# Start of a decoder trunk step: more filler products, another buffer for two loads, an earlier gather

## The chip, the cores and the metric

The kernel runs on one core of one Trainium2 chip. The metric is the device time of one execution in microseconds (us); less is better. The kernel before has a median of 1006.9 us over three runs (1005.82 to 1008.11).

## The reference

One layer of a hybrid decoder is run for a prompt of 512 tokens and for 8 samples of one token each; both share the weights. All is float32.

```python
def trunk_layer(x, c, conv_buf, h0, pos0, attend, ...):
    sh1, sc1, g1, sh2, sc2, g2 = ada_modulation(c, ada_w, ada_b)      # silu(c) @ ada_w + ada_b, six parts
    h = rms_norm(x, norm1_g) * (1.0 + sc1) + sh1
    z = h @ w_in
    xr, gr, q, k, v, fl, ga, gb = jnp.split(z, cuts, axis=-1)
    ...   # branch A: convolution, RG-LRU, gelu gate, @ w_proj_a
    logf = jax.nn.log_sigmoid((fl + b_f).astype(jnp.float32))
    yb = attend(q, k, v, logf).reshape(B, T, ATTN_W) @ w_proj_b       # samples: cache_logf[page_table] too
    x = x + g1 * ((sigmoid(ga) * ya + sigmoid(gb) * yb) @ w_o)
    ...   # second norm, SwiGLU, residual; final norm
```

The model width D is 1024, the feed-forward width 2816, 16 heads of 64. The samples attend to 1024 past rows each, in pages of 128 rows; `cache_logf` is gathered by the page table.

## The kernel before, in words

Activations lie transposed: eight tiles of 128 features by 520 columns (512 prompt tokens, 8 samples), called `x[f]`, `xn[f]` (normed), `h[f]` (modulated). A full-precision product is made of three TensorE products, since each operand is split in a high and a low part (`whi`/`wlo` for weights, `hh`/`hl` for h): ScalarE rounds the high part, VectorE subtracts for the low one. TensorE then runs through one long list of such products; weights come by DMA in chunks and are split ahead of their use.

Instructions are written in program order, and a scheduler of the framework orders each engine's queue from it, by its own model of when operands are ready; each engine then works through its queue in that fixed order and waits at its head. All weight loads go through SyncE's (SP's) queue.

The start, which the change touches, is in this order:

- SP loads `par1` (norm and conditioning rows), the eight tiles of x, some constants, and then the adaLN weights. The modulation of the first norm is made in three parts (`first_mod`, parts 0, 1, 2: features 0 and 1, 2 and 3, 4 to 7). Parts 0 and 1 take four tiles each, two row blocks (`kq`) per tile; part 2 takes eight loads, one per row block.
- The sum of squares: for each f ScalarE squares `x[f]` (line 594) and VectorE adds it to `sq` (line 596). Ten products with one column each (`ss`, line 604) sum over the partitions; then come a root, a reciprocal, five small diagonal tiles `dg` (line 610), the products that spread the reciprocal over all partitions (`r`, line 615), and the copies of it to `r1`.
- Beside the squares `keep_busy` issues filler products into a bank that nobody reads (`idle`, line 509): ones times `x[f]`, 260 columns, float32, which the chip runs as two matmul instructions each. Each waits for the one before, and for the load of `x[f]`.
- `first_mod(0)` (line 489) stands on TensorE in two halves, ahead of and behind the products for `r`. Then `first_mod_end(0)`: copy, transpose (followed by two more fillers), `mod`, `n1amp`. Then `first_h(0)` and the first query products (`qa`, line 574).
- Parts 1 and 2 of the modulation follow between query products (lines 489 and 502), and `first_h(4)` to `first_h(7)` come after the end of part 2. Each `first_h` has two small operations on GpSimd (POOL) for the 8 sample columns (lines 538 and 539).

Three pools of buffers matter. `pgp` has 7 tiles of 4 KB per partition; nearly all early loads use it. `wp` with tag `wraw` has 2 tiles of 8 KB per partition, taken in turn: first two for query weights (`qraw`), the third for the last two row blocks of part 2 (`both`), the fourth for `lfp` (the gathered log f of the past), the fifth for the first weight chunk. `heap` has 60 tiles of 520 columns, handed out by `slot`.

`past_load` (line 439) is an indirect DMA, issued by POOL: it gathers 64 rows of the log f cache by `idx`, which a small DMA loads from the page table; `ptb` is the same table for page loads. The gathered rows are used by the transposes `lft` (line 451) in `past_turn`.

Of the kernel before, what the change touches and what calls it, by code (L numbers as in the profile page):

```python
# [67 lines left out]
def kernel(ctx, tc, xT, par1, par, gates, b_f, cst, cse, own, cache_k, cache_v, cache_lf, pt,  # L68
# [3 lines left out]
    pe, act, dve, pool, sp = nc.tensor, nc.scalar, nc.vector, nc.gpsimd, nc.sync  # L72
# [9 lines left out]
    def slot(name, cols=NT, dt=F32, parts=128):  # L82
        return heap.tile([parts, cols], dt, name=name, tag="slot")

    def bank(name, parts=128, cols=512):
        return psp.tile([parts, cols], F32, name=name, tag="bank")
# [76 lines left out]
    for jt in range(FF // 128):  # L163
        c = len(chunks)
# [4 lines left out]
        for name in BLOCKS:  # L169
            units.append((c, name, 4))  # L170
            if name in JOIN[jt]:
                g, i = JOIN[jt][name]
# [32 lines left out]
    def load_chunks(upto):  # L205
        while state["dma"] < len(chunks) and state["dma"] <= upto:
            c = state["dma"]
            if c in joined:
                raw = pgp.tile([128, GROUP, 256], F32, name="wraw", tag="pg")
            else:  # L210
                raw = wp.tile([128, KT, 256], F32, name="wraw", tag="wraw", bufs=2)
            o = 0
            for src, r0, nk, c0, n in chunks[c]:
                sp.dma_start(raw[:, :nk, o:o + n],
                             src[r0:r0 + nk * 128, c0:c0 + n].rearrange("(k p) c -> p k c", p=128))
                o += n
            raws[c] = raw
            state["dma"] += 1
# [214 lines left out]
    ptb = keep.tile([1, NS * NPAGE], I32, name="ptb")  # L433
    idx = keep.tile([NS * NPAGE, 1], I32, name="idx")
    lfp = []

    def past_load():
        t = wp.tile([NS * NPAGE, 2048], F32, name="lfp", tag="wraw", bufs=2)
        pool.indirect_dma_start(out=t, out_offset=None, in_=cache_lf,
                                in_offset=bass.IndirectOffsetOnAxis(ap=idx[:, 0:1], axis=0),  # L440
                                bounds_check=NPOOL - 1)
        lfp.append(t.rearrange("p (k h) -> p h k", h=H))
# [36 lines left out]
    def first_mod(part, acc, kqs):  # L479
        if part < 2:  # L480
            for kq in range(kqs[0], kqs[-1], 2):
                raw = pgp.tile([128, 2, 512], F32, name="araw", tag="pg")
                for v in range(2):
                    c0 = 1024 * v + 256 * part
                    sp.dma_start(raw[:, :, 256 * v:256 * v + 256],
                                 ada_w[kq * 128:kq * 128 + 256, c0:c0 + 256].rearrange("(k p) c -> p k c", p=128))
                for k in range(2):
                    for g in range(4):
                        m = pe.matmul(acc[32 * g:32 * g + 32, :128], lhsT=silc[:, kq + k],
                                      rhs=raw[:, k, 128 * g:128 * g + 128],  # L490
                                      start=kq + k == 0, stop=kq + k == KT - 1, tile_position=(0, 32 * g))
            return
        for kq in kqs:
            if kq < 6:
                raw = pgp.tile([128, 2, 512], F32, name="araw", tag="pg")
            else:
                if kq == 6:
                    both = wraw().rearrange("p (a k) c -> p a (k c)", a=2)
                raw = both[:, kq - 6].rearrange("p (v c) -> p v c", v=2)
            sp.dma_start(raw, ada_w[kq * 128:kq * 128 + 128, :2048].rearrange("p (v c) -> p v c", v=2)[:, :, 512:])  # L500
            for g in range(4):
                pe.matmul(acc[32 * g:32 * g + 32, :256], lhsT=silc[:, kq],
                          rhs=raw[:, g // 2, 256 * (g % 2):256 * (g % 2) + 256],
                          start=kq == 0, stop=kq == KT - 1, tile_position=(0, 32 * g))

    def keep_busy(m, n, f=0):
        for _ in range(n):
            with tc.issue_after(m.ins) if m is not None else nullcontext():
                m = pe.matmul(idle[:, :HALF], lhsT=ones, rhs=x[f][:, :HALF], start=True, stop=True)
        return m  # L510

    def first_mod_end(part, acc):
        nb = 1 if part < 2 else 2
        sb = slot("adas", 256)
        mods = act.copy(sb[:, :128 * nb], acc[:, :128 * nb])
        tp = bank(f"adaft{part}")
        for b in range(nb):
            m = pe.transpose(tp[:, b * 128:b * 128 + 128], sb[:, b * 128:b * 128 + 128], ident)
        if part == 0:
            keep_busy(m, 2)  # L520
        f0, nf = ((0, 2), (2, 2), (4, 4))[part]
        fs = slice(f0, f0 + nf)
        tv = tp[:, :128 * nb].rearrange("p (b g c) -> p b g c", b=nb, g=4)
        for v in (1, 0):
            dve.tensor_tensor(
                mod[:, v, fs].rearrange("p (q b) c -> p b q c", b=nb), tv[:, :, 2 * v:2 * v + 2, 0:9],
                prm1[:, fs, P_AB + v:P_AB + v + 1].rearrange("p (q b) c -> p b q c", b=nb).to_broadcast([128, nb, 2, 9]),
                ALU.add)
        amps = dve.scalar_tensor_tensor(amp1[:, fs], mod[:, 1, fs], 1.0,
                                        prm1[:, fs, P_N1:P_N1 + 1].to_broadcast([128, nf, 9]), ALU.add, ALU.mult)  # L530
        return mods, amps
# [21 lines left out]
    def q_split(kp, raw, g3, behind=(), mid=None):  # L553
        hi = wp.tile([128, 2, 384], F32R, name="whi", tag="whi", bufs=3)
        lo = wp.tile([128, 2, 384], F32R, name="wlo", tag="wlo", bufs=3)
        with ExitStack() as st:
            for b in behind:
                st.enter_context(tc.issue_after(b.ins))
            for k in range(0, 2, 1 if mid else 2):
                ks = slice(k, k + 1 if mid else 2)  # L560
                state["act"] = act.copy(hi[:, ks], raw[:, ks])
                if k:
                    st.enter_context(tc.issue_after(mid()[1].ins))
                state["last"] = dve.tensor_tensor(lo[:, ks], raw[:, ks], hi[:, ks].bitcast(F32), ALU.subtract)
        for k in range(2):
            for n in range(3):
                qw[2 * kp + k, g3 + n] = hi[:, k, 128 * n:128 * n + 128], lo[:, k, 128 * n:128 * n + 128]
# [9 lines left out]
    def wraw():  # L577
        return wp.tile([128, KT, 256], F32, name="wraw", tag="wraw", bufs=2)
# [6 lines left out]
    def q_step(ks, g3, k, banks, n0=0, n1=6):  # L585
        for n in range(n0, n1):
            q_matmuls(ks, g3 + n // 2, n % 2, k, banks[n])
# [4 lines left out]
    for f in range(KT):  # L592
        t = slot("sq1")
        act.activation(t, x[f], AF.Square)
        if f:
            dve.tensor_tensor(sq, sq, t, ALU.add)
        else:
            sq = t
        if 0 < f < 6:
            m = keep_busy(m, 1, f)  # L600
    NB = NT // 5
    ps = bank("ss1", NB, 5)
# [6 lines left out]
    for b in range(5):  # L609
        dve.tensor_scalar(dg[:, NB * b:NB * b + NB], ident[:NB, :NB], rt[:, b:b + 1], None, ALU.mult)  # L610
    first_mod(0, acc[0], range(0, 4))
    r1 = slot("r1")
    for j, (t0, t1) in enumerate(((0, 3 * NB), (3 * NB, NT))):
        ps = bank(f"r1_{j}")[:, :t1 - t0]
        pe.matmul(ps, lhsT=ones[:NB, :], rhs=dg[:, t0:t1], start=True, stop=True)
        act.copy(r1[:, t0:t1], ps)
    first_mod(0, acc[0], range(4, KT))
    qraw = {}

# [21 lines left out]
    q_step((0, 1), 0, 0, banks)  # L641
    q_step((0, 1), 0, 1, banks)
    first_mod(1, acc[1], range(0, 4))
    for n in range(6):
        t0, t1 = HALVES[n % 2]
# [22 lines left out]
    banks = [bank(f"qc{i}_{j}") for i in range(3) for j in range(2)]  # L668
    q_step(range(2, KT), 0, 2, banks)
    first_mod(2, acc[2], range(6, 8))  # L670
    q_split(2, qraw[2, 0], 0)
    first_mod_end(2, acc[2])
    q_step(range(2, KT), 0, 3, banks)
# [7 lines left out]
        q_step(range(2, KT), 0, k, banks)  # L681
    qbanks = banks
    sp.dma_start(prm, par)
    sp.dma_start(ptb, pt.rearrange("a b -> (a b)")[None, :])
    sp.dma_start(idx, pt.rearrange("a (b c) -> (a b) c", c=1))
    for kp in (2, 3):
        q_loads(kp, 3)
        q_split(kp, qraw[kp, 3], 3, ends)
    past_load()
    load_chunks(0)  # L690
    flr = slot("flr", KT * 32).rearrange("p (k c) -> p k c", k=KT)
    pool.memset(flr, 0.0)
# [332 lines left out]
    for i in range(KT):  # L1025
        if i % 4 == 0:
            qtp.append(bank(f"qt{i}", NS))
        if i < 6:
            t = qpart[i]
            for j, (t0, t1) in enumerate(HALVES):  # L1030
                if i < 3:
                    b = qbanks[2 * i + j]
                else:
                    b = bank(f"q{i}_{j}")
# [57 lines left out]
    g = [None] * KT  # L1092
# [397 lines left out]
    g = None  # L1490
# [340 lines left out]
    for j in range(2):  # L1831
        for m in range(2 * PLAIN):
            if j == 0:
                begin(u + 3)
            b = bank(f"fi{m}_{j}")
# [90 lines left out]
```

## Time and profile before

| what | value |
|---|---|
| median of three runs | 1006.9 us (1005.82 to 1008.11) |
| the profiled execution's own time | 1008.05 us |
| its span, first to last instruction | 1006.4 us |
| PE (TensorE) busy | 987.9 us, 98% |
| DVE (VectorE) busy | 789.2 us, 78% |
| ACT (ScalarE) busy | 566.2 us, 56% |
| POOL busy | 340.0 us, 34% |
| HBM read and written | 203 GB/s over the span |

Some 1.65 us of the execution's time lie outside the span. Busy time of PE is the union of its matmuls as the profile models them, so 98% says that it hardly stood still, not that it ran at its peak.

### The profile page before, as it was taken

What the parts mean: (1) busy time and instruction counts of PE and PEld (TensorE: products, weight loads), DVE (VectorE), ACT (ScalarE), POOL (GpSimd) and SP (SyncE); (2) the same over time, 40 slices, a digit from 0 to 9 for tenths busy, and PEclk for the clock granted to TensorE, in tenths of its full rate; (3) what the DMA queues carried; (4) which work ended last, traced back from release to release, by engine and by line L of the source; (5) the groups of instructions that cost most, each with busy time, mean ns of one, the idle gap of its engine ahead of it and who ended that gap; (6) DMA issues with size and microseconds to landing.
All of it is one profiled execution on the core that took longest, in us unless ns stands there. A gap on an engine that the chain in (4) does not pass through costs nothing.

```text
span 1006.4 us, 21548 instructions
## 1 busy us (share of the span) xinstructions
PE 987.9 (98%) x8090; PEld 917.0 (91%) x8090; DVE 789.2 (78%) x1410; ACT 566.2 (56%) x1165; POOL 340.0 (34%) x436
## 2 busy tenths in 40 slices
PE   6999999999999999999999999999999999999997
PEld 5899999999898988888888888999999999999996
DVE  4488999979999888887665454869888888888864
ACT  5443779876952477777782233554444444445453
POOL 0163121323244255644400001494343442433212
PEclk9999999999999999999999999999999999999999
DMA  9898756889879999997767995333324243233222
GB/s 320 294 291 300 230 198 183 272 260 304 266 237 371 321 312 279 320 283 235 250 208 260 334 338 151 86 97 93 106 84 126 66 125 100 69 106 105 64 63 86
DMA packets 165883, 206.14 MB, mean 205 GB/s; under 512 B 9986, under 2 KB 128402, under 8 KB 165714
## 3 DMA queue, kind: packets, MB, share of 16 engines
q1 hardware_dynamic: 149538, 153.24, 49.0%
q0 software_dynamic: 12560, 45.10, 13.2%
q10 hardware_dynamic: 3680, 6.42, 1.7%
q8 instruction: 63, 1.03, 0.4%
q14 instruction: 42, 0.34, 0.1%
HBM read 191.64 MB, written 13.09 MB: 203 GB/s over the span
## 4 chain that ended last, share of the span: by engine, by line
PE 87%; ACT 5%; DVE 4%; issue 2%; DMA 1%; POOL 0%; SPq 0%; DVEq 0%; POOLq 0%; ACTq 0%
PE fo L311 13%; PE wo L311 5%; PE pb L311 4%; PE gb L311 4%; PE k L311 4%; PE ga L311 4%; PE v L311 4%; PE xr L311 3%; PE pa L311 3%; PE pv L942 3%; PE gr L311 2%; PE po L1415 2%; PE ada L378 2%; PE ptt L1381 2%; PE fi L311 1%
## 5 line engine op out<-in xcount | busy, mean ns | idle before, releaser
L250 ACT CAST whi<-wraw 128x1024 fp32r<-128x1024 f32 (+1 forms) x79 | 82.2, 1040 | 97.5 <-PE pb L311 34.5
L252 DVE TENSOR_TENSOR wlo<-wraw,whi 128x1024 fp32r<-128x1024 f32 (+1 forms) x79 | 99.7, 1262 | 19.7 <-ACT whi L250 17.4
L274 ACT CAST wb<-ws 128x512 fp32r<-128x512 f32 x72 | 44.8, 622 | 88.9 <-PE fo L311 61.9
L311 PE MATMUL fo<-ach,wb 128*128 128x260 f32 x512 | 93.3, 282 | 0.0
L311 PEld LDWEIGHTS fo<-ach,wb 128*128 128x128 f32 x512 | 78.9, 188 | 0.0
L275 DVE TENSOR_TENSOR wb<-wraw,wb 128x512 fp32r<-128x512 f32 x86 | 74.5, 866 | 4.9 <-ACT wb L274 4.0
L265 POOL TENSOR_TENSOR ws<-wraw 128x512 f32<-128x512 f32 x18 | 23.8, 1324 | 152.9 <-DMA wraw<-in_w_fi_dram 94.8
L311 PE MATMUL fo<-acl,wb 128*128 128x260 f32 x256 | 72.3, 282 | 0.0
L275 DVE TENSOR_TENSOR wb<-ws,wb 128x512 fp32r<-128x512 f32 x72 | 61.1, 849 | 13.9 <-ACT wb L274 12.4
L274 ACT CAST wb<-wraw 128x512 fp32r<-128x512 f32 x86 | 53.5, 623 | 32.2 <-ACT cp L1813 6.2
L790 POOL DMA_DIRECT2D pg<-in_cache_k_dram x70 | 37.8, 540 | 100.2 <-DVE S L854 54.7
L853 DVE TENSOR_TENSOR pg<-pg,qb 128x1024 f32<-128x1024 f32 x48 | 57.6, 1214 | 1.4 <-DMA pg<-in_cache_k_dram 1.4
L854 DVE TENSOR_REDUCE S<-pg 128x16 f32<-128x1024 f32 x48 | 57.3, 1207 | 0.2
L1372 POOL TENSOR_SCALAR p<-p,mu 128x128 f32<-128x128 f32 (+3 forms) x28 | 38.4, 1380 | 55.8 <-DVE mu L1368 26.6
L311 PEld LDWEIGHTS fo<-acl,wb 128*128 128x128 f32 x256 | 48.2, 188 | 0.0
L1366 ACT ACTIVATE p<-p,mu 128x128 f32<-128x128 f32 (+3 forms) x64 | 35.3, 553 | 18.9 <-DVE mu L1365 18.6
L311 PE MATMUL v<-hh,whi 128*128 128x260 f32 x128 | 37.4, 292 | 1.0 <-DVE S L910 0.5
L311 PE MATMUL k<-hh,whi 128*128 128x260 f32 x128 | 37.3, 292 | 0.0
L311 PE MATMUL pb<-oh,whi 128*128 128x260 f32 x128 | 37.1, 290 | 0.2 <-ACT oh L1473 0.2
L311 PE MATMUL gb<-hh,whi 128*128 128x260 f32 x128 | 37.3, 291 | 0.0
L311 PE MATMUL ga<-hh,whi 128*128 128x260 f32 x128 | 36.6, 286 | 0.6 <-ACT tA L1188 0.6
L311 PE MATMUL pa<-gh,wlo 128*128 128x260 f32 x128 | 36.3, 284 | 0.8 <-DVE wlo L252 0.8
(1131 smaller groups left out, 3961.4 us busy)
## 6 DMA issues: line engine op xcount, KB each, us to landing
wraw<-in_w_fi_dram SPq DMA_DIRECT2D x44, 512.0 KB, 4.1
pg<-in_cache_k_dram POOLq DMA_DIRECT2D x42, 512.0 KB, 5.6
pg<-in_cache_v_dram SPq DMA_DIRECT2D x42, 512.0 KB, 5.9
araw<-in_ada_w_dram SPq DMA_DIRECT2D x38, 512.0 KB, 7.0
wraw<-in_w_in_dram SPq DMA_DIRECT2D x28, 512.0 KB, 6.7
wraw<-in_w_in_dram SPq DMA_DIRECT2D x11, 1024.0 KB, 8.7
pg<-in_cache_v_dram POOLq DMA_DIRECT2D x22, 512.0 KB, 6.4
wraw<-in_w_fo_dram SPq DMA_DIRECT2D x16, 512.0 KB, 4.4
```

What stands on the lines that cost most here:

```text
L250: state["act"] = act.copy(hi[:, :k1 - k0], src)
L252: state["last"] = dve.tensor_tensor(lo[:, :k1 - k0], src, hi[:, :k1 - k0].bitcast(F32), ALU.subtract)
L265: pool.tensor_tensor(s1, a21, a22, ALU.add)
L274: state["act"] = act.copy(t[:, :4], src)
L275: state["last"] = dve.tensor_tensor(t[:, 4:], src, t[:, :4].bitcast(F32), ALU.subtract)
L311: state["mm"] = pe.matmul(out[:, :t1 - t0], lhsT=wt[k], rhs=at, start=k == 0 and m == 0, stop=k == nk - 1 and m == 2)
L790: done.append(eng.dma_start(pg, cache[bass.ds(r, 1), :, c0:c1].rearrange("a p c -> (a p) c")))
L853: dve.tensor_tensor(pg, pg, q, ALU.mult)
L854: last = dve.tensor_reduce(S[r // 2][:, c:c + H], pg.rearrange("p (h d) -> p h d", d=DH), AX.X, ALU.add)
L942: pe.matmul(pv[0][32 * gq:32 * gq + 32, :], lhsT=pw[r][:, c:c + 32], rhs=pgs[gq // 2][:, 512 * hf:512 * hf + 512], start=j == 0, stop=j == ...
L1366: act.activation(p[:, :n + 128], p[:, :n + 128], AF.Exp, bias=mu[:, 0:1], scale=-1.0, accum_out=mu[:, 1:2])
L1372: (pool.tensor_scalar(p, p, mu[:, 2:3], None, ALU.mult) if a and i + 1 < KT else act.activation(p, p, AF.Copy, scale=mu[:, 2:3]))
```

## The change

Three edits, all in the first 50 us or so of the program.

1. The fillers beside the squares are issued for f = 2 to 7 instead of f = 1 to 5.
2. The loads of the last two row blocks (kq 6 and 7) of part 2 go to four `slot` tiles of 512 columns, one for each half, instead of the two halves of a `wraw` tile. So there are four DMAs of 256 KB instead of two of 512 KB, and `wraw` has one taker less.
3. The loads of `ptb` and `idx` and the gather `past_load` stand right after these loads in the program, ahead of the end of part 2 and of `first_h(4)` to `first_h(7)`; before, they stood after `first_h(7)` and the loads of the last query weights.

```diff
         for kq in kqs:
+            src = ada_w[kq * 128:kq * 128 + 128, :2048].rearrange("p (v c) -> p v c", v=2)[:, :, 512:]
             if kq < 6:
                 raw = pgp.tile([128, 2, 512], F32, name="araw", tag="pg")
+                sp.dma_start(raw, src)
+                raw = [raw[:, v] for v in range(2)]
             else:
-                if kq == 6:
-                    both = wraw().rearrange("p (a k) c -> p a (k c)", a=2)
-                raw = both[:, kq - 6].rearrange("p (v c) -> p v c", v=2)
-            sp.dma_start(raw, ada_w[kq * 128:kq * 128 + 128, :2048].rearrange("p (v c) -> p v c", v=2)[:, :, 512:])
+                raw = [slot("araw", 512) for v in range(2)]
+                for v in range(2):
+                    sp.dma_start(raw[v], src[:, v])
             for g in range(4):
                 pe.matmul(acc[32 * g:32 * g + 32, :256], lhsT=silc[:, kq],
-                          rhs=raw[:, g // 2, 256 * (g % 2):256 * (g % 2) + 256],
+                          rhs=raw[g // 2][:, 256 * (g % 2):256 * (g % 2) + 256],
                           start=kq == 0, stop=kq == KT - 1, tile_position=(0, 32 * g))
...
-        if 0 < f < 6:
+        if f > 1:
             m = keep_busy(m, 1, f)
...
     first_mod(2, acc[2], range(6, 8))
+    sp.dma_start(ptb, pt.rearrange("a b -> (a b)")[None, :])
+    sp.dma_start(idx, pt.rearrange("a (b c) -> (a b) c", c=1))
+    past_load()
     q_split(2, qraw[2, 0], 0)
...
     sp.dma_start(prm, par)
-    sp.dma_start(ptb, pt.rearrange("a b -> (a b)")[None, :])
-    sp.dma_start(idx, pt.rearrange("a (b c) -> (a b) c", c=1))
     for kp in (2, 3):
         q_loads(kp, 3)
         q_split(kp, qraw[kp, 3], 3, ends)
-    past_load()
     load_chunks(0)
```

## Rows read from the trace of the kernel before

**Rows 1.** The page: busy time of each engine, and the chain by engine.

```profile
PE 987.9 (98%) x8090; PEld 917.0 (91%) x8090; DVE 789.2 (78%) x1410; ACT 566.2 (56%) x1165; POOL 340.0 (34%) x436
PE 87%; ACT 5%; DVE 4%; issue 2%; DMA 1%; POOL 0%; SPq 0%; DVEq 0%; POOLq 0%; ACTq 0%
```

**Rows 2.** Waits of PE over the whole run: us in total, times, longest.

```profile
PE idle L509 <- DMA x<-in_xT_dram: 5.5, 2, 5.1
PE ss L604 <- DVE sq L596: 1.6, 1, 1.6
...
PE pa L311 <- DVE wlo L252: 0.8, 2, 0.5
```

**Rows 3.** Timeline of PE to 21.5: start, us, instruction, count, idle before.

```profile
6.65 3.83 PE L509 MATMUL idle<-x,cs 128*128 128x260 f32 x8 [0.39 <-DMA x<-in_xT_dram]
12.08 1.90 PE L604 MATMUL ss<-cs,sq 128*104 128x1 f32 x10 [1.59 <-DVE sq L596]
13.91 2.34 PE L489 MATMUL adaf<-araw,silc 128*32 128x128 f32 x34
16.18 2.10 PE L615 MATMUL r<-dg,cs 104*128 104x312 f32 x4
18.21 1.21 PE L489 MATMUL adaf<-araw,silc 128*32 128x128 f32 x30
...
19.96 1.04 PE L509 MATMUL idle<-x,cs 128*128 128x260 f32 x4
21.24 0.39 PE L574 MATMUL qa<-hh,whi 128*128 128x260 f32 x1 [0.24 <-ACT hh L537]
```

**Rows 4.** Line 509, the fillers: duration of one in ns, least, median, most.

```profile
L509 PE MATMUL idle<-x,cs x14: 382/641/799, 5.1 to 20.6; 128*128 128x260 f32 x14
```

**Rows 5.** The chain in order of time: start, us, what.

```profile
19.75 0.82 ACT whi L561 x2
...
20.59 1.09 ACT hh L537 x2
...
21.82 4.43 PE qa L574 x34
...
27.82 0.99 PE adaf L489 x26
...
43.75 1.00 PE adaf L502 x16
...
45.68 10.51 PE qc L574 x86
```

**Rows 6.** Timeline of all engines, 12 to 24: the diagonal tiles on VectorE.

```profile
14.54 1.01 DVE L610 TENSOR_SCALAR dg<-cs,rt 104x104 f32<-104x104 f32 x5
```

**Rows 7.** Stretches: length, PE, PEld, DVE, ACT, POOL busy, clock, DMA share, GB/s.

```profile
10.00:15.00 5.00, 3.40 (x36) 2.82 (x38) 2.47 (x7) 2.19 (x3) 0.00 (x0) 1.00 1.10 356
...
40.00:45.00 5.00, 5.00 (x56) 3.56 (x55) 0.96 (x1) 1.71 (x5) 0.00 (x0) 1.00 0.45 149
...
100.00:900.00 800.00, 796.72 (x6466) 738.15 (x6465) 647.58 (x1119) 470.19 (x964) 280.04 (x335) 1.00 0.66 209
```

**Rows 8.** DMA issues at 10.04, 11.02, 18.41, 31.60, 35.60, in order: us to landing.

```profile
araw<-in_ada_w_dram SPq DMA_DIRECT2D x1, 256.0 KB, 5.5
...
wraw<-in_w_in_dram SPq DMA_DIRECT2D x1, 384.0 KB, 6.3
...
araw<-in_ada_w_dram SPq DMA_DIRECT2D x1, 256.0 KB, 6.4
...
wraw<-in_ada_w_dram SPq DMA_DIRECT2D x1, 512.0 KB, 9.1
...
idx<-in_pt_dram SPq DMA_DIRECT2D x1, 0.2 KB, 6.9
```

**Rows 9.** Timeline of POOL, 46 to 50: h's sample columns and the gather.

```profile
46.23 0.20 POOL L538 TENSOR_TENSOR hr<-xn,n1amp 128x8 f32<-128x8 f32 x1 [12.52 <-DVE n1amp L529]
...
47.55 1.32 POOL L439 DMA_INDIRECT lfp<-in_cache_lf_dram,idx  x1 [0.77 <-ACT hh L541]
```

## The prediction, written before the change was run

> **What bounds the kernel now.** I read the page first [rows 1]: PE is busy for 98% of the span and the chain that ended last runs for 87% on PE. So time is won only where PE waits, or where it runs at the slow one of its two levels. The waits of PE over the whole run [rows 2] are few: about 5 us before its first filler, where x has to arrive, 1.6 us until the squares are summed, and then nothing over 0.9 us in one place. A change that frees a buffer or a queue in the stretch after 22 us therefore has no wait to remove; the start is where to look.
>
> The timeline of PE's start [rows 3] shows the pace. Eight filler instructions take 3.83 us from 6.65, four of the same kind take 1.04 us from 19.96, and single ones last from 382 to 799 ns, 641 in the middle [rows 4]. Spaced by what is left after the last one's own time, the late four start every (1.04 - 0.38) / 3 = 0.22 us; the early ones, with 0.64 us for the last, every 0.43 us where no load holds them up (my estimate; (3.83 - 0.64) / 7 = 0.46 with the one pause in it). That is the factor of two between 1.2 and 2.4 GHz. The same holds for the modulation products: 34 in 2.34 us from 13.91, 30 in 1.21 us from 18.21. So everything up to about 18.4 us ran at the slow level, and PE had stood still for 1.59 us ahead of `ss`. From 21.82 the chain is on PE without a break [rows 5]. The end of the kernel is thus this start plus a fixed amount of PE work.
>
> **Edit 1, fillers for f = 2 to 7.** Five fillers (ten instructions) become six (twelve); the one at 5 us goes, two come behind. Cost at the slow level: the first can start at 6.65 as now, so twelve are spent at 6.65 + 12 x 0.43 = 11.8 us. `ss` can't start before 12.08, since VectorE's last sum ends there [rows 3]. The cover is 0.25 us; without it, a filler too many would cost what reaches past 12.08, at most 0.43 us for one instruction. ScalarE and VectorE don't wait for fillers. So its price is nothing, and the idle 1.59 us ahead of `ss` shrink to about 0.25.
>
> What it can give is the fast level from about 12 us on instead of 18.4. Bounds: nothing, if the clock rises where it does now; at most the whole difference of rates. Step by step, with the clock up at 12.08. `ss`: 1.90 to about 1.0, so the root and the rest follow 0.9 us earlier, and `dg`, which ended at 14.54 + 1.01 = 15.55 [rows 6], ends at 14.65. `r` no longer stands behind slow modulation products (the first half falls from 2.34 to about 1.2 and ends near 14.3): it starts at about 14.4 instead of 16.18 and takes some 1.05 instead of 2.10. So `r1` is ready 2.8 us earlier.
>
> Then loads decide. The DMA engines are full in this stretch, share 1.10 at 356 GB/s [rows 7], and PE's pace doesn't move them. The load issued at 10.04 lands 5.5 us later, at 15.5; the last one of part 0, 256 KB behind it, at 15.5 + 0.75 = 16.3; the first query weights, issued at 11.02, at 17.3 [rows 8]. The second half of the modulation can thus end at about 16.3 + 0.7 = 17.0 instead of 18.21 + 1.21 = 19.42, which is 2.4 earlier, and the weights' casts on ScalarE start at 17.35 instead of 19.64 or so: they and the copy ahead of them ended at 20.57, and the first `hh` follows at 20.59 [rows 5]. 17.35 + 0.93 for two casts gives 18.3 for `hh`, so the unbroken stretch starts **2.3 us earlier**. I take this value; its ends are 0 and 2.8.
>
> Is it given back? I compare each later load with its use, 2.3 us earlier. The last load of part 1 lands at 18.41 + 6.4 = 24.8, used from 27.82, then 25.5: it holds by 0.7. The last of part 2 lands at 31.60 + 9.1 = 40.7, used at 43.75, then 41.4: it holds by 0.7 as well [rows 5, 8]. Nothing comes due closer than that, and from 43 us the DMA engines have room (share 0.45 over 40 to 45, [rows 7]). Beyond 50 us I can't follow each wait; the listed ones of the middle (0.8 us for `pa` on VectorE the largest, [rows 2]) could each grow or shrink by a few tenths.
>
> **Edit 2, slots for kq 6 and 7.** Two DMAs of 512 KB become four of 256 KB: two more issues on SP of some 0.4 us, while 9 us of transfers are queued ahead (31.60 to 40.7), so nothing. The same bytes land at the same time, at 40.7. What follows: `lfp` takes an earlier `wraw` tile, and the first weight chunk no longer waits for the products of 43.75; it is loaded some 6 us earlier, into the idle DMA time after 43 us. No PE wait hangs on it, so I count 0. On the other side, a slot might not be free; the bound is SP's queue standing behind it until a reader is done, and 3 us of stand cost nothing by the slack above.
>
> **Edit 3, the gather.** On SP `ptb` and `idx` come ahead of the loads of the last query weights: two tiny issues of 0.3 and 1.1 us. `idx` landed 6.9 us after its issue at 35.60, at 42.5 [rows 8]; issued some 2 us earlier behind kq 7 it lands at about 41. The gather holds POOL for 1.32 us [rows 9], and it now stands ahead of `first_h(4)`, where before it fell between that one and `first_h(5)`. Queued behind it are eight small POOL operations, and behind them the copies of the sample columns and so `hh` of tiles 4 to 7. The gather at 41.0 to 42.4 is done before `n1amp` of part 2 is there (46.2, then 43.9), so it costs nothing, and tiles 5 to 7 get their POOL operations 1.3 us sooner. PE doesn't wait for them now (10.51 us without a break from 45.68, [rows 5]), so I count 0; the gain is bounded by 0.3 us of such waits as edit 1 might open.
>
> The Trainium skill (Trainium Kernel Development and Optimization, Key Constraints) says that the queues of SP, ACT and POOL share the same 16 DMA engines: by it the earlier gather takes time from the query weights behind `idx`. The stretch after 40 us, with a share of 0.45, agrees that there is room for it.
>
> **Sum.** 1008.05 - 2.3 = 1005.75 us for an execution that starts as slowly as the profiled one. That one lies 1.15 above the median of 1006.9. If the three runs' spread has nothing to do with the start, the median falls by all of it, to 1004.6; if the spread is the start, the median falls to 1005.75 at best. I forecast between, **1005.0 us**, own range 1004.0 to 1006.0.
>
> **Rivals.**
>
> *The clock varies from run to run.* Three runs of the same program spread by 2.3 us, 1005.82 to 1008.11, which is just what the slow start costs by the sum above. Then the fastest run may already have risen before `ss`, and the middle one in part; the change only makes this frequent, and the median goes to 1006.9 - 0.5, some 1006.4, no measurable change. Against it: the profiled execution is at the fast level only after 18 us although the fillers ran for 3.83 us. The Trainium skill (TensorE: Matmul & The Clock Gate, Part 1: The HAM clock gate) says that the slow level is the default, that activity lifts it, and that the look at activity isn't aligned with the kernel's start, so that one kernel shows different numbers of slow products; one trace can't show this, and the spread agrees with it. Chance 0.19.
>
> *Later waits shrink too.* With POOL and the first chunk earlier, half of the middle's pauses (800 - 796.7 = 3.3 us from 100 to 900, [rows 7]) go as well: 1005.0 - 1.6 = 1003.4. Nothing ties those waits to the first 50 us. Chance 0.12.
>
> *The gather blocks POOL: slower.* If `idx` lands late, POOL's head waits for it and PE starves at tile 4. PE needs `hh` of tile 4 at about 47.4 now (two thirds of a step of 18 products after 45.68), 45.1 after the shift; POOL takes 0.55 us for it (46.23 to 47.55, less 0.77 of idle, [rows 9]) and ScalarE's copy some 0.2 more, an estimate from the sizes. So the gather has to end by 44.3; this costs the whole gain when it ends at 46.6, with `idx` at 45.3, and turns slower from there. A landing at 46.9 gives 1006.9 + 1.6 = 1008.5. For it: the full queue, and an order that a scheduler may also upset elsewhere. Against it: an issue that is earlier than the one which landed at 42.5. Chance 0.13.
>
> **How the numbers follow.** Forecast 0.56. A measurement of this kernel tells some 0.2% (2 us) from no change, so faster means below 1004.9: half of the forecast's chance (0.28) and the third case (0.12) give 0.40; the other half with the first rival (0.19) 0.47; slower 0.13. The range 1003.3 to 1007.2 holds the forecast and both rivals below; what it leaves out is the slower case and a little of the middle.
>
> **What would show it.** Right: no pause over 0.4 us between the fillers and `ss`; ten `ss` in about 1.0 us; `r` at half its time; the first `qa` at about 19.0; the gather on POOL near 41; the chunk's load near 39. Wrong: `ss` still 1.9 us long; fillers running past 12.1; a PE wait on `hh` or on `araw` between 24 and 50 us; or the early start present and new waits of 2 us later.

## The result and the profile after

The changed kernel has a median of 1008.97 us over 15 runs (1007.2 to 1010.41), the kernel before 1007.12 over 15 (1005.49 to 1008.11). The ratio is 1.0018, 95% interval 1.0011 to 1.0026: slower by 1.1 us at the least, and outside my range. Here and below, medians leave out the three executions whose mean granted clock was far lower (1067.55 us of the kernel before, 1822.36 of best_fillers, 1066.02 of whole_rfirst2). Yet the one profiled execution has a span of 1006.1 us against 1006.4, and took 1008.98. Two things have to be read apart: what happens in the span, and what lies outside.

TensorE's waits after (us in total, times, longest) answer [rows 2]:

```profile
PE idle L511 <- DMA x<-in_xT_dram: 6.7, 1, 6.7
...
PE ss L606 <- DVE sq L598: 0.9, 1, 0.9
...
PE qa L576 <- ACT hh L539: 0.6, 1, 0.6
...
PE adaf L489 <- DMA araw<-in_ada_w_dram: 0.3, 1, 0.3
PE qc L576 <- ACT hh L539: 0.3, 1, 0.3
```

Two waits are new, each 0.3 us: modulation products on a load, and query products on `hh`. The timeline of PE's start after (start, us, instruction, count, idle before) answers [rows 3]:

```profile
6.67 4.46 PE L511 MATMUL idle<-x,cs 128*128 128x260 f32 x12 [6.67 <-DMA x<-in_xT_dram]
12.00 1.08 PE L606 MATMUL ss<-cs,sq 128*104 128x1 f32 x10 [0.87 <-DVE sq L598]
13.01 1.29 PE L489 MATMUL adaf<-araw,silc 128*32 128x128 f32 x36
14.62 1.18 PE L489 MATMUL adaf<-araw,silc 128*32 128x128 f32 x14 [0.32 <-DMA araw<-in_ada_w_dram]
15.72 1.14 PE L617 MATMUL r<-dg,cs 104*128 104x312 f32 x4
...
19.57 0.39 PE L576 MATMUL qa<-hh,whi 128*128 128x260 f32 x1 [0.55 <-ACT hh L539]
```

Edit 1 does what it says here. The fillers end at 11.1 already and the shortest takes 0.38 us, so the clock rose among them; the pause ahead of `ss` is 0.87 us, not the 0.25 that I had worked out at the slow pace. `ss` takes 1.08 instead of 1.90, `r` 1.14 instead of 2.10, and the first query product is 1.67 us earlier (21.24 to 19.57). This lead, the time by which PE is ahead of the kernel before at the same product, is kept to 39.72, where the third query step starts, which was at 41.39 before:

```profile
41.39 2.36 PE qc L574 x18
```

Then it goes. The chain in order of time after (start, us, what) answers the last lines of [rows 5]:

```profile
39.72 2.36 PE qc L576 x18
42.08 0.57 PE adaf L504 x8
42.65 0.44 PE qc L576 x2
43.09 0.56 PE adaf L504 x4
43.65 0.56 PE qc L576 x3
44.20 0.56 PE adaf L504 x4
44.76 0.68 PE qc L576 x4
45.44 0.25 PE adaft L520 x2
...
46.17 0.82 ACT hh L539
...
47.04 8.92 PE qc L576 x72
```

Before, the 16 products of row blocks 6 and 7 were one block of 1.00 us from 43.75, 4 query products followed, and 86 were left at 45.68, which brings the last 72 to 47.35. After, the same 16 come in blocks of 8, 4 and 4, with 2 and 3 query products between. They take 0.57 + 0.56 + 0.56 = 1.69 us, and 2 and 3 query products take 0.44 and 0.56 instead of 0.24 and 0.36 at the usual 0.12 each. That is 1.1 us for crossing over from one kind of product to the other and back twice more. Five query products more are done by 45.44, but part 2 of the modulation ends when it ended before, so `hh` of tile 4 is late for PE by 0.3. At 47.04 the lead is 0.3 us; the first `lft` comes at 59.09 instead of 59.34.

Outside the span: the kernel before has 1.59 to 1.72 us there in each of 91 executions. The changed one has 1.60 to 1.96 in 11 of 15 and 2.88 to 3.48 in 4, the profiled one among them (2.88). The DMA view of the profile after, from 1005 to 1010 us, shows one transfer of instructions, past the last output. In the eleven other profiles read here, with 1.63 to 1.82 us outside the span, there is none after 1000 us:

```profile
DMA packets 1, 0.02 MB, mean 3 GB/s; under 512 B 0, under 2 KB 0, under 8 KB 0
q8 instruction: 1, 0.02, 1.2%
```

The gather did what I said: issued at 40.38, done 4.32 us before POOL's next work was ready (timeline of POOL after, as [rows 9]).

```profile
40.38 1.53 POOL L439 DMA_INDIRECT lfp<-in_cache_lf_dram,idx  x1 [8.34 <-DMA qraw<-in_w_in_dram]
46.23 0.19 POOL L540 TENSOR_TENSOR hr<-xn,n1amp 128x8 f32<-128x8 f32 x1 [4.32 <-DVE n1amp L531]
```

### The profile page after: what moved, and what is told of

It is laid out like the page before. It is cut to its first block, busy times and chain, and to the rows that moved or that the text cites. A ratio compares the mean times of both kernels' runs of the same rounds, so it can differ in the third digit from the quotient of the medians.

```text
span 1006.1 us, 21556 instructions
## 1 busy us (share of the span) xinstructions
PE 986.6 (98%) x8092; PEld 915.6 (91%) x8092; DVE 791.0 (79%) x1410; ACT 565.4 (56%) x1165; POOL 338.3 (34%) x436
## 3 DMA queue, kind: packets, MB, share of 16 engines
q8 instruction: 63, 1.03, 0.4%
## 4 chain that ended last, share of the span: by engine, by line
PE 90%; ACT 4%; DMA 3%; DVE 1%; issue 1%; SPq 1%; POOL 0%; POOLq 0%; DVEq 0%; ACTq 0%
PE fo L311 13%; PE wo L311 5%; PE gb L311 5%; PE xr L311 5%; PE pb L311 4%; PE k L311 4%; PE ga L311 4%; PE v L311 4%; PE gr L311 3%; PE pa L311 3%; PE pv L944 3%; PE po L1417 2%; PE ada L378 2%; PE ptt L1383 2%; PE fi L311 1%; PE qc L576 1%
## 5 line engine op out<-in xcount | busy, mean ns | idle before, releaser
L275 DVE TENSOR_TENSOR wb<-ws,wb 128x512 fp32r<-128x512 f32 x72 | 64.1, 891 | 13.5 <-ACT wb L274 11.8
```

Of the source, the lines that this page charges most:

```text
L275: state["last"] = dve.tensor_tensor(t[:, 4:], src, t[:, :4].bitcast(F32), ALU.subtract)
```

## The experiments

Three theories were open. *Cut order*: the new loads make the scheduler cut the 16 products on TensorE, and that costs the lead. *Traffic* or *buffers*: the gather, the early chunk or the slots' loads cost something by themselves. *Code tail*: it is the time outside the span, which ends late in some executions. Each kernel is compared with runs of the kernel before on its own chip. In the table, "products together" means that the 16 products are held as one run on TensorE; "both orders" means that `r` is held ahead of the second half of part 0 as well.

| run | what it has | median us | ratio to before, 95% interval | median span |
|---|---|---|---|---|
| changed kernel | edits 1, 2, 3 | 1008.97 | 1.0018 (1.0011 to 1.0026) | 1006.7 |
| fillers_only | edit 1 | 1007.57 | 1.0002 (0.9993 to 1.0010) | 1005.65 |
| slots_only | edit 2 | 1010.36 | 1.0030 (1.0017 to 1.0044) | 1008.7 |
| gather_only | edit 3 | 1007.07 | 1.0000 (0.9990 to 1.0009) | 1005.4 |
| after_whole | 1, 2, 3, products together | 1006.97 | 0.9995 (0.9986 to 1.0003) | 1004.9 |
| slots_whole | 2, products together | 1007.97 | 1.0008 (0.9999 to 1.0017) | 1006.3 |
| fillers_whole | 1, products together | 1005.97 | 0.9989 (0.9980 to 0.9998) | 1004.3 |
| whole_rfirst | 1, 2, 3, both orders | 1005.25 | 0.9983 (0.9974 to 0.9992) | 1003.6 |
| whole_rfirst2 | the same again | 1005.51 | 0.9986 (0.9977 to 0.9995) | 1003.9 |
| best_fillers | 1, both orders | 1005.24 | 0.9984 (0.9974 to 0.9995) | 1003.6 |
| best_gather | 1, 3, both orders | 1005.64 | 0.9989 (0.9980 to 0.9998) | 1004.0 |
| no_fillers | none of them, no fillers at all | 1007.55 | 1.0008 (0.9999 to 1.0016) | 1005.9 |

The kernel before has 1007.18 on the chip of fillers_only, slots_only, gather_only and after_whole, 1006.95 on that of slots_whole, fillers_whole, whole_rfirst and no_fillers, and 1006.91 on that of the other three. Differences between runs of different chips are taken below from each run's difference to the kernel before on its chip.

**fillers_only**, the edit at line 599 alone.

```diff
-        if 0 < f < 6:
+        if f > 1:
```

> Edit 1 alone (fillers f = 2 to 7). In the changed kernel's profile the first query product came 1.7 us earlier than before, and by 47 us only 0.3 us of that was left, because the scheduler cut the 16 modulation products of row blocks 6 and 7 into pieces of 8, 4 and 4 with query products between them. Theory 'cut order': here the order on TensorE cuts them in only two pieces (8 and 8), so a part of the start's gain is left: 0.5 to 1.0 us under the kernel before, some 1006.3 us. Rival 'traffic' (the earlier gather and chunk load do the harm): without them all of the 1.7 us is left, 1005.4. Rival 'code tail' (a last block of TensorE's instructions is fetched after the last output in the changed kernel's profile, at 1008.4 us, and the time outside the span is 2.9 instead of 1.65): TensorE has two instructions more than before, so the tail shows here too in some executions, and the median is 1007 to 1007.5.

Measured 1007.57, no change. Its order cuts the 16 products as well, in 8 and 8 with 5 query products between:

```profile
42.10 0.57 PE adaf L502 x8
42.67 0.80 PE qc L574 x5
43.47 0.57 PE adaf L502 x8
```

That the new fillers shift the scheduler's own reckoning of time, and the order with it, is my reading; no run shows the reckoning. I had expected a smaller loss; in its profile the lead falls from 1.66 at the first query product to 0.71 us at the first `lft`. The tail shows in 1 of 12.

**slots_only**, edit 2 alone (the first hunk of the change).

> Edit 2 alone (four loads of 256 KB into slots). 'Cut order': the order on TensorE has the 16 products of row blocks 6 and 7 cut into 8, 4 and 4 while the start is the old one, so this is the harmful part: 1.0 to 1.5 us over the kernel before, 1008.1 to 1008.6 us. 'Traffic': the first weight chunk comes early but the gather does not; about half of the loss, 1007.8. 'Code tail': TensorE's queue is as long as in the changed kernel, so some executions show 3 us outside the span instead of 1.65, and the spans by themselves are no longer than before.

Measured 1010.36, 3.2 over the kernel before: more than any theory had. All 7 executions have 1.63 to 1.71 outside the span, so the code tail isn't it. In its profile, which starts as slowly as the one before, PE is 1.8 us late at the first `lft` (61.13 against 59.34). Of this 0.2 us is not the cut itself: PE waits for `qp`, and the chain runs there over the gather, which still stands late on POOL (49.31). The rest came later and isn't tied to this place: 0.6 us near 310 us in a longer wait for a value page, 0.7 from there to the end in a slightly slower pace, which gather_only's profile shows too.

**gather_only**, edit 3 alone (the last two hunks).

> Edit 3 alone (page table loads and gather ahead of tiles 4 to 7). TensorE's order through row blocks 6 and 7 is that of the kernel before. 'Cut order': no change, within 0.3 us of the kernel before (1006.8 to 1007.4 us). 'Traffic': slower by 1 us or more, 1008.1 us. 'Code tail': no change, since TensorE's queue is as long as before.

Measured 1007.07: 'traffic' by the gather falls. Its profile held a surprise, the start with the old fillers (timeline of PE; then stretches with length, busy PE, PEld, DVE, ACT, POOL, granted clock, DMA share, GB/s):

```profile
5.09 4.67 PE L509 MATMUL idle<-x,cs 128*128 128x260 f32 x10 [5.09 <-DMA x<-in_xT_dram]
11.71 1.07 PE L604 MATMUL ss<-cs,sq 128*104 128x1 f32 x10 [1.96 <-DVE sq L596]
12.72 2.34 PE L489 MATMUL adaf<-araw,silc 128*32 128x128 f32 x34
...
19.48 0.39 PE L574 MATMUL qa<-hh,whi 128*128 128x260 f32 x1 [0.24 <-ACT hh L537]
```

```profile
9.50:12.50 3.00, 1.04 (x11) 0.79 (x9) 1.95 (x3) 1.99 (x3) 0.00 (x0) 1.00 1.09 364
13.00:16.00 3.00, 3.00 (x36) 2.27 (x29) 1.20 (x6) 0.09 (x1) 0.00 (x0) 0.50 1.09 355
16.50:20.00 3.50, 2.87 (x38) 1.84 (x37) 2.62 (x7) 2.79 (x9) 0.99 (x3) 1.00 1.09 356
```

The clock was up for `ss` (1.07 us), fell to 1.2 GHz after PE had stood still for 1.96 us and then done ten products of one column, and rose again by 16.5. The first query product came at 19.48, earlier than in the changed kernel. (Ahead of the first change that was recorded the column shows 1.00 whatever the pace, so there the pace has to be read.)

**after_whole**: all edits, but the next query step is queued on TensorE behind the last product of row block 7 (`tc.issue_after`). The same edit makes slots_whole of slots_only and fillers_whole of fillers_only.

```diff
             for g in range(4):
-                pe.matmul(acc[32 * g:32 * g + 32, :256], lhsT=silc[:, kq],
+                state["ada"] = pe.matmul(acc[32 * g:32 * g + 32, :256], lhsT=silc[:, kq],
...
     first_mod_end(2, acc[2])
-    q_step(range(2, KT), 0, 3, banks)
+    with tc.issue_after(state["ada"].ins):
+        q_step(range(2, KT), 0, 3, banks)
```

> All three edits, but the query step behind row blocks 6 and 7 is queued behind their last product, so that the 16 products stay together as in the kernel before; TensorE's queue is as long as before. 'Cut order': the start's gain is kept, 1.0 to 1.7 us under the kernel before, 1005.4 to 1006.1 us. 'Traffic': still slower than the kernel before, 1008.5 us. 'Code tail': the tail is gone, 0.4 us better than the changed kernel in the middle, spans as there: 1008.5 us.

Measured 1006.97, 2.1 better than the changed kernel when each is set against the kernel before on its chip, with loads, slots and gather unchanged; two of 12 executions still had the tail. The chain of its profile has the block whole again:

```profile
39.70 2.36 PE qc L576 x18
42.06 1.00 PE adaf L504 x16
43.06 0.67 PE qc L576 x4
43.73 0.26 PE adaft L520 x2
43.99 10.34 PE qc L576 x86
```

86 products are left at 43.99 instead of 45.68: the lead of 1.7 us passes through. The first `lft` comes 1.6 us ahead of the changed kernel's (57.48 against 59.09), from starts within 0.02. So the cut is what cost the changed kernel its lead. But I had expected 1.0 to 1.7 us under the kernel before, and 0.2 were measured, with an interval that holds no change. Hence the next four.

**slots_whole**

> Edit 2 alone, but with the products of row blocks 6 and 7 kept together on TensorE as in the kernel before. 'Cut order': the whole 3.2 us that edit 2 alone cost are gone: within 0.4 us of the kernel before, 1006.7 to 1007.5 us. Rival 'buffers' (the loads in slots, or the first weight chunk that moves forward by 6 us, cost something of their own): a good part of the 3.2 us is left, 1008.5 us or more.

Measured 1007.97: 2.2 of the 3.2 us are gone. What is left, 1.0, isn't clear of no change.

**fillers_whole**

> Edit 1 alone, with the products of row blocks 6 and 7 kept together. If the clock often rises early with the old fillers too ('clock varies'), the new ones gain only in the executions in which it did not: 0.2 to 0.8 us under the kernel before, 1006.3 to 1006.9 us. If the kernel before nearly always starts slowly, all of the 1.7 us is gained: 1005.4 us.

Measured 1005.97, 1.0 under the kernel before and 1.4 better than fillers_only, from which it differs by the order alone: the cleanest measure of the cut, here of one crossing more. In the two profiles the first `lft` is 0.9 apart (57.73 and 58.63).

**whole_rfirst**: after_whole, and the second half of part 0 queued behind `r`.

```diff
-        pe.matmul(ps, lhsT=ones[:NB, :], rhs=dg[:, t0:t1], start=True, stop=True)
+        m = pe.matmul(ps, lhsT=ones[:NB, :], rhs=dg[:, t0:t1], start=True, stop=True)
         act.copy(r1[:, t0:t1], ps)
-    first_mod(0, acc[0], range(4, KT))
+    with tc.issue_after(m.ins):
+        first_mod(0, acc[0], range(4, KT))
```

> All edits, row blocks 6 and 7 kept together, and the second half of part 0's modulation products queued behind the two products that spread the reciprocal root (in the changed kernel's profile 25 of 32 stood ahead of them, waited 0.3 us for a load, and the spreading began at 15.7 us). Now it begins at about 14.4, and the first query product at about 19.0 instead of 19.55: 0.3 to 0.7 us under the version without this (1006.97), 1006.3 to 1006.7 us. Rival: the last load of part 0 and the weights' casts set the start anyway: no change, 1007.0 us.

Measured 1005.25, beyond what I expected. The timeline of PE in its profile:

```profile
12.87 1.08 PE L489 MATMUL adaf<-araw,silc 128*32 128x128 f32 x32
14.20 1.14 PE L617 MATMUL r<-dg,cs 104*128 104x312 f32 x4 [0.25 <-DVE dg L612]
15.27 1.50 PE L489 MATMUL adaf<-araw,silc 128*32 128x128 f32 x32
...
18.65 0.39 PE L576 MATMUL qa<-hh,whi 128*128 128x260 f32 x1 [0.31 <-ACT hh L539]
```

`r` starts at 14.20 and the first query product at 18.65, 0.9 us ahead of after_whole's. The medians differ by 1.5; what the other 0.6 are, no run separates.

**no_fillers**: `if False:` in place of the condition, on the kernel before.

> The kernel before without any filler beside the squares. 'Clock varies': the old fillers brought an early rise in a part of the executions, so without them all start slowly; 0.5 to 1.5 us over the kernel before, 1007.6 to 1008.6 us, and spans that scatter less. If the old fillers never lifted the clock ahead of the sum of squares: no change, 1007.1 us.

Measured 1007.55, 0.6 over the kernel before, with an interval that holds no change, and spans that scatter much as before (1004.0 to 1007.5): it doesn't decide between the two. Its profile starts slowly (`ss` takes 1.86 us):

```profile
11.98 1.86 PE L604 MATMUL ss<-cs,sq 128*104 128x1 f32 x10 [11.98 <-DVE sq L596]
```

**best_fillers, best_gather, whole_rfirst2**: whether edits 2 and 3 cost anything once both orders are held. The first leaves out edits 2 and 3, the second edit 2.

> Edit 1 with both orders on TensorE (row blocks 6 and 7 together, the spreading of the root ahead of part 0's second half), without edits 2 and 3. If edits 2 and 3 cost something of their own beside the cut ('buffers': all edits with the order kept were at 1006.97, edit 1 alone with it at 1005.97), this one is under the version with all edits: 1004.3 to 1005.0 us. If not, the two are equal, 1005.2 to 1005.6 us. Either way 1.5 to 2.8 us under the kernel before.

> Edits 1 and 3 with both orders, without edit 2. Edit 3 alone changed nothing (1007.07 against 1007.18), so this is within 0.4 us of the version with edit 1 only: 1004.5 to 1005.5 us. If the gather costs something once the start is early (it then meets the last query weights in the DMA queues), 0.8 us more than that version.

> All three edits with both orders, once more and beside the two above: 1005.2 us as before, within 0.5. If it is 0.7 us or more above the version with edit 1 alone, the slots' loads cost that much by themselves ('buffers'); if less than 0.4, the difference seen between the other versions was one of chips.

Measured side by side on one chip 1005.24, 1005.64 and 1005.51. 'Buffers' falls for this version: with both orders held, edits 2 and 3 neither cost nor bring anything that shows. With only the products held together it stays open: there edit 2 stands 1.0 us above the kernel before (slots_whole), and all edits 0.8 behind edit 1 alone (after_whole, fillers_whole). All three beat the kernel before, by 1.3 to 1.7 us, and so the changed kernel too; edit 1 with the two orders is enough.

## Why the prediction was wrong

*Where PE is bound* was right: nothing after 50 us mattered, the start and what follows on PE decided.

*Edit 1* was right in its mechanism: `ss` in 1.08 us (I said about 1.0), `r` in 1.14 (1.05), no cost at the fillers' end. What I priced at nothing and was not: edit 1 by itself also changes the order and cuts the 16 products in two (fillers_only). And its size was off twice. In the trace the shift was 1.67 instead of 2.3 us: `r` began at 15.72, not at 14.4, since the order now had 25 of part 0's 32 products ahead of `r` in place of 17, and they waited for a load. I had taken the old order as fixed; with it held at 16 the first query product came 2.59 earlier (whole_rfirst). And not every execution of the kernel before starts as slowly as the one I read. Of four profiled starts with the old fillers two were slow (the kernel before, slots_only) and two had the clock up before `ss` (gather_only, slots_whole). The mean granted clock of an execution hints at how often: it is 0.998 in those two slow starts, and 0.995 in the two that rose early and fell back. Of 91 executions of the kernel before, 39 have 0.995 or less (median span 1005.1 us), 33 have 0.996 (1005.0) and only 19 have 0.997 or 0.998 (1006.4). So the execution that my sum starts from seems to be of the rarer, slower kind; this isn't proof, since no_fillers' slow start has 0.996. That is the first rival, to which I gave 0.19. What edit 1 brings in the median, with the products together, is 1.0 us (fillers_whole), not the 1.9 between 1006.9 and my 1005.0.

*Edit 2* is the step that failed: "two more issues on SP of some 0.4 us, while 9 us of transfers are queued ahead (31.60 to 40.7), so nothing". The loads themselves were never waited for. But with four loads in place of two, the 16 products came in blocks of 8, 4 and 4 on TensorE, with query products between them; that the scheduler does this by each load's own moment of readiness is my reading. Holding the order took back 2.1 us in the changed kernel, 2.2 in slots_only and 1.4 in fillers_only. I compared loads with uses and queues with waits, and never asked whether the order on the bounding engine would stay: "is it given back?" was answered by loads alone. The one sign of being wrong that came was small, a wait of 0.3 us on `hh`; the cut shows as no wait at all, since PE stays busy.

*Edit 3* was right: no cost (ratio 1.0000, interval 0.9990 to 1.0009), none of POOL's work behind the gather late. The room that I saw in the DMA engines after 40 us was gone, with the first weight chunk issued at 38.1 instead of 44.8 (share 1.06 over 40 to 45 us in the changed kernel, 0.45 before), but no PE wait came of it. The slower rival that I built on it named the wrong place; 0.13 for slower was too little, because it priced one mechanism and no reordering.

*Given back later* was right in its bounds: row block 7's loads and part 1's were never waited for, and the middle moved by tenths up to 300 us. Near 310 us single executions win or lose up to 1.5 us at one wait for a value page (no_fillers' profile gains 1.5 there on the kernel before); it scatters over kernels of all sorts.

*Outside the span* my sum left the 1.65 us as they were. In the kernel before they are fixed; with the new fillers 8 of 93 executions had 2.9 to 3.6. In the changed kernel, where 4 of 15 had it, it adds some tenths to the median of the time. Spans alone, 1006.7 against 1005.5 (1007.12 less 1.65), make 1.2 of the 1.85 us; the rest is this tail and the scatter of both. What decides when the last block of instructions comes late stays open: kernels of almost the same length differ.

Also open: what a crossing between the modulation's products and query products costs inside TensorE. The rows show blocks of 4 and of 8 taking the same 0.56 us where 16 take 1.00; no run varied the block alone. And of the 2.1 us that the order costs in the changed kernel, the profiles account for 1.6 by the first `lft` (1.1 for crossings and 0.3 for the wait among them); the rest lies within what two medians of this scatter can differ by.

## What to carry to other kernels

Under a scheduler that orders by its own reckoning, an edit that costs nothing where it stands can reorder the engine that bounds: lay the queue of that engine before and after side by side, and hold the order that matters explicitly. Here a run of small products of another shape was best kept together, and splitting its loads split the run. Read a start that depends on the clock from several executions, not from one trace, before pricing what a faster start is worth.

## What the runs showed of the hardware

With twelve filler instructions the clock came up before `ss` in all seven profiles that have them: the shortest filler takes 0.38 us in each. With ten it came up in two of four; in the kernel before and in slots_only none takes less than 0.64. In gather_only it was lost again after 1.96 us of standstill and ten products of one column (granted clock 0.50 from 13 to 16 us, though PE was busy throughout). With fillers up to the sum the pause ahead of `ss` was 0.87 us in the changed kernel and 0.28 in whole_rfirst, and neither profile shows a fall there. But that isn't safe either: in fillers_whole's profile, with the same fillers and a pause of 1.03 us, the clock falls at 12.5 and is up again at about 16 (stretches with the columns as above):

```profile
11.00:12.50 1.50, 1.06 (x14) 1.05 (x18) 0.39 (x1) 0.52 (x1) 0.00 (x0) 1.00 1.09 356
...
13.00:15.50 2.50, 2.50 (x46) 2.06 (x38) 1.05 (x6) 0.00 (x0) 0.00 (x0) 0.50 1.10 353
15.50:17.00 1.50, 1.50 (x13) 0.98 (x15) 0.00 (x0) 0.41 (x2) 0.00 (x0) 0.85 1.06 369
```

With the same fillers the first query product came at 21.24 (the kernel before) and 19.48 (gather_only), or at 21.21 (slots_only) and 20.17 (slots_whole). Not all of that is the clock: `ss` starts between 11.71 and 12.38 in these four.
